# Keys and queries of the next heads transposed ahead of a step's projection matmuls, in a hybrid attention layer

## The chip, the core and the metric

The kernel runs on one core of a Trainium2 chip. The metric is the device time of one execution in microseconds (us), the median over runs. A core has a tensor engine (PE) with a queue for its weight loads (PEld), a vector engine (DVE), a scalar engine (ACT), GpSimd (POOL) and SyncE (SP), which here only issues transfers (DMAs). Each works through its own list of instructions in order and waits for the others by semaphores. PE writes its products into PSUM, eight banks of 128 x 512 float32; DVE and ACT read them from there.

## The reference

One layer of a transformer over 512 tokens of width 1024, in float32:

```python
x = x + 0.5 * swiglu_ffn(x, g1, ...)
h = rms_norm(x, g_mix)
(fq, fk, fv, ff, dq, dk, dv, iq, ik, iw, ga, gb) = split_columns(h @ w_in)
# branch A, 8 heads of 64 (FoX): q, k normed per head,
#   softmax(q.k / 8 + decay of the forget gates, causal) @ v
# branch B, 8 heads of 64 (DSA), one shared key and value head: the same with a relative bias,
#   over the 128 keys that an indexer (iq, ik, iw) picks for each query
merged = sigmoid(ga) * (o_a @ w_branch_a) + sigmoid(gb) * (o_b @ w_branch_b)
x = x + merged @ w_out
x = x + 0.5 * swiglu_ffn(x, g2, ...)
```

## The kernel before

The time goes through five stages: the first feed-forward block, the head of the projection by `w_in` with the indexer's scores, the sixteen attention heads, the merge with `w_out`, and the second feed-forward block. A float32 product is made from three matmuls on operands split in a high and a low part (`mm3`, lines 141 to 143: high times high, low times high, high times low). The high part is a cast on ACT, the low part a difference on DVE.

The order of PE's instructions is the order in which the code is written (`manual_schedule` for PE). The order on ACT, DVE, POOL and SP is set by a scheduler that simulates the program as it is built; so a change in PE's order may change theirs. The scheduler also deals out the tiles to the banks of a tag.

The attention loop (line 1011) goes over 16 heads g: 0 to 7 are FoX, 8 to 15 DSA. A head has four steps s, one for each block of 128 queries, the longest block (512 keys) first. A step holds, in order on PE:

- `value_step` (line 919), for an earlier head's probabilities: `flip` transposes up to four 128x128 tiles p into the PSUM tile pt (L886), ACT casts it to ph (L890), DVE writes the low part pl (L891); then `weigh` multiplies the ph and pl of the flip before with the values (L896, L897).
- `softmax_block` (line 868): scores ps_qk (L579, L580); DVE adds the bias and takes the minimum mn (L875), ACT makes the exponential (L877), DVE the reciprocal rs (L878), POOL scales p (L879).
- `prod.run(FILL[g], ...)`: the fill, some two us of matmuls of the rest of the projection (and, in later heads, of the branch product and the gates), written as units that give up control every few matmuls. Weights are cast to wh (L130) and wl (L136) for it. A finished unit is read out of PSUM: normed queries and keys kn (L650 on ACT, then L546, L548, L549, and POOL), values fv (L663, L664), branch products, gates.
- behind the fill: `get_bias` of the next head (a DMA on SP, L943) at s = 0, and, at odd heads only, `get_k` of the next pair of heads at s = 0 and `get_q` at s = 1.

`get_k` (line 924) does anything only for the heads below 8, so at g = 1, 3 and 5 (and once ahead of the loop). It transposes four tiles kn into the PSUM tile ps_k (L557), and for each half of 64 partitions ACT writes kh (L540) and DVE kl (L541), and two DMAs on SP (L937) copy them to the other 64 partitions. `get_q` does it at g = 1, 3, ..., 13: four transposes into ps_q (L557), and for each half ACT writes st (L570) and DVE the other half of st (L571). In both, ACT and DVE take turns on the one tile: the first half's DVE instruction is over before ACT starts on the second half.

PSUM is full: three banks of tag "acc" for the products, two of tag "s" for the scores, one for the outputs po ("pv"), and two of tag "pt", in which ps_k, ps_q and all the pt of the flips take turns.

Of the kernel before, what the change touches and what calls it, by code (L numbers as in the profile page):

```python
# [35 lines left out]
H = 8  # L36
# [15 lines left out]
def tile_hybrid_layer(ctx: ExitStack, tc: tile.TileContext, a: dict):  # L52
# [467 lines left out]
    with (tc.tile_pool(name="mix", bufs=1) as mp, ExitStack() as att_ctx,  # L520
# [18 lines left out]
        def evac_split(ps, g, hi, lo):  # L539
            S.mul(hi, ps, g)  # L540
            V.scalar_tensor_tensor(lo, ps, g, hi.bitcast(F32), op0=OP.mult, op1=OP.subtract)  # L541
# [18 lines left out]
        def stack_split(ps, g, nm):  # L560

            out = []
            for hf in range(2):
                own, oth = slice(hf * DH, hf * DH + DH), slice(DH - hf * DH, P - hf * DH)
                st = at.tile([P, T], F32R, tag=nm[hf], bufs=2, name="st")
                if g is None:
                    S.copy(st[own], ps[own])
                    V.tensor_sub(st[oth], ps[own], st[own].bitcast(F32))
                else:
                    S.mul(st[own], ps[own], g[own])  # L570
                    V.scalar_tensor_tensor(st[oth], ps[own], g[own], st[own].bitcast(F32),  # L571
                                           op0=OP.mult, op1=OP.subtract)
                out.append(st)
            return out

        def stack_mm(out, st, k, i, n):

            b = slice(i * P, (i + 1) * P)
            PE.matmul(out[:, :n], st[:, b], k[0][:, :n], start=True, stop=False)  # L579
            PE.matmul(out[:, :n], st[:, b], k[1][:, :n], start=False, stop=True)  # L580
# [256 lines left out]
        def topk_run(n):  # L837

            nonlocal topk_debt
            topk_debt += n  # L840
            with tc.issue_after(anchor[0].ins) if anchor[0] else nullcontext():
                while topk_debt >= 1:
                    next(topk, 0)
                    topk_debt -= 1
# [23 lines left out]
        def softmax_block(g, i, q, k, bias, pr, st):  # L868
            n = P * (i + 1)
            b = bias(i)  # L870
            ps = psum.tile([P, T], F32, tag="s", bufs=2, name="ps_qk")
            stack_mm(ps, q[g % 2], k[g % 2], i, n)
            p = at.tile([P, n], F32, tag=f"p{i}", bufs=2, name="p")
            mn, rs = st[0][:, i:i + 1], st[1][:, i:i + 1]
            anchor[0] = V.tensor_tensor_reduce(out=p, in0=ps[:, :n], in1=b, scale=1.0, scalar=3e38,  # L875
                                               op0=OP.add, op1=OP.min, accum_out=mn)
            S.activation(p, p, AF.Exp, bias=mn, scale=-1.0, accum_out=rs)  # L877
            V.reciprocal(rs, rs)  # L878
            G.tensor_scalar(p, p, rs, 1.0, op0=OP.mult, op1=OP.mult)  # L879
            pr[i] = p  # L880
# [32 lines left out]
        def columns(tiles, c, name):  # L913
            return transposed(lambda t: tiles[t // 2][:, t % 2, c * P:(c + 1) * P], name)

        def get_q(g):

            nm, c = ("fq", g // 2) if g < H else ("dq", g // 2 - 4)
            prod.finish(upto[f"{nm}{c // 2}"])
            gain = gq[:, 0:1] if g < H else gq[:, 1:2]  # L920
            return stack_split(columns(tn[f"{nm}{c // 2}"], c % 2, "ps_q"), gain, ("qh", "ql"))

        def get_k(g):

            if g >= H:
                return [(dkh, dkl)] * 2
            c = g // 2
            prod.finish(upto[f"fk{c // 2}"])
            ps = columns(tn[f"fk{c // 2}"], c % 2, "ps_k")
            gain = hg[:, 2:3]  # L930
            out = []
            for hf in range(2):
                own, oth = slice(hf * DH, hf * DH + DH), slice(DH - hf * DH, P - hf * DH)
                hi, lo = k = [mp.tile([P, T], F32R, tag=tag, bufs=3, name=tag) for tag in ("kh", "kl")]
                evac_split(ps[own], gain[own], hi[own], lo[own])
                for t in k:
                    nc.sync.dma_start(t[oth].bitcast(F32), t[own].bitcast(F32))  # L937
                out.append(k)
            return out

        def get_bias(g):
            cb = at.tile([P, T], F32, tag="cb", bufs=2, name="cb")
            nc.sync.dma_start(cb, cum_rows[g:g + 1, :].to_broadcast([P, T]) if g < H else a["rel"][g - H])  # L943

            def bias(i):
                n = P * (i + 1)
                b = tmp_tile("b")
                if g < H:
                    G.tensor_scalar(b[:, :n], cb[:, :n], 1.0, ncum[:, i, g:g + 1], op0=OP.mult, op1=OP.add)
                    G.affine_select(out=b[:, i * P:n], in_=b[:, i * P:n], compare_op=OP.is_ge, fill=BIG, base=0,  # L950
                                    pattern=[[-1, P]], channel_multiplier=1)
                else:
                    G.tensor_sub(b[:, :n], sc[i] if i else cpos, cb[:, T - n:T])
                return b[:, :n]
            return bias
# [6 lines left out]
        for step in range(30):  # L962
            prod.run(MM, upto["fv0"])
            topk_run(TOPK_PRE)
            if step == 5:
                nk = get_k(0)
            if step == 10:
                next(later[1], 0)
            if step == 15:
                nq = get_q(0)  # L970
# [10 lines left out]
        def value_step(g, j):  # L981

            nonlocal flipped, po
            new = (g, j, *flip(j, probs[g])) if g < 2 * H else None
            if flipped:
                fg, fj, ph, pl = flipped
                if fj == 0:

                    po = acc_tile("po") if fg > H and fg % 2 else psum.tile([P, T], F32, tag="pv", name="po")
                if fg < H:  # L990
                    if fj == 0 and fg == 4:
                        prod.finish(upto["fv1"])
                    weigh(po, fj, fv[fj, fg // 4][:, fg % 4], ph, pl)
                else:
                    weigh(po, fj, dvv[:, fj], ph, pl)
                if fj == NT - 1:
                    if fg in (H, H + 2):

                        if fg > H:
                            prod.finish(upto["ba7"])  # L1000
                        for part, nm in zip(oB, ("oh", "ol")):
                            part += [mp.tile([P, T], F32R, tag=f"{nm}{c}", name="oB") for c in range(1, 4)] if fg > H else [
                                mp.tile([P, T], F32R, tag="k" + nm[1], bufs=3, name="oB")]
                    head_out(fg, po, oA if fg < H else oB)
            flipped = new

        def limit(g, s):

            return upto["dq1"] if g < 6 else upto["ga7"] if 4 * g + s < 4 * 9 + 2 else len(units)

        for g in range(2 * H):
            q, k, bias = nq, nk, nb
            probs[g] = [None] * NT
            st = [small.tile([P, NT], F32, tag=nm, name=nm) for nm in ("mn", "rs")]
            for s in range(NT):
                vg, vj = (g - 1, s - 1) if s else (g - 2, NT - 1)
                if vg >= 0:
                    value_step(vg, vj)
                topk_run(TOPK_BEAT)
                softmax_block(g, NT - 1 - s, q, k, bias, probs[g], st)  # L1020
                prod.run(FILL[g], limit(g, s))
                topk_run(TOPK_BEAT)
                if g == H - 1 and s == NT - 1:
                    for _ in topk:
                        pass
                if g + 1 < 2 * H:
                    if s == 0:
                        nb = get_bias(g + 1)
                    if s == 0 and g % 2:
                        nk = get_k(g + 1)  # L1030
                    if s == 1 and g % 2:
                        nq = get_q(g + 1)
                if g == 2 * H - 2:
                    ga[s] = mp.tile([P, T], F32, tag="tn", bufs=8, name="ga")
                    nc.sync.dma_start(ga[s], kept[:, s])
# [127 lines left out]
```

## Time and profile before

| | |
|---|---|
| median of 3 runs | 1089.55 us (1089.39 to 1089.67) |
| span of the profiled execution | 1087.8 us |
| instructions in it | 17784 |
| PE's clock as granted | 9 tenths or more in each of the 40 slices |
| DMA, mean over the span | 118 GB/s |

The page gives only a span for the profiled execution, from its first instruction to its last; the runs' times also hold what lies around it, 1089.55 - 1087.8 = 1.75 us if the profiled execution was like the median one. In a row of a time line stand the start, the duration, the engine, the line, the operation, output and inputs, partitions by elements and the count; in brackets how long the engine was idle before it and what ended the wait. In a row of the waits stand the total in us, the number of times and the longest. Matmuls are pipelined: the next starts before the one before has ended, so a duration of 0.28 us for a 256-wide matmul goes with a start every 0.12 us.

### The profile page before, as it was taken

To read this page: it belongs to the slowest core of one execution; us is meant where nothing else is said; L and a number is where in the kernel's file an instruction comes from. 1 tells how busy PE (TensorE), PEld (TensorE's weight loads), DVE (VectorE), ACT (ScalarE), POOL (GpSimd) and SP (SyncE) were. 2 spreads that over 40 slices of the span, in tenths; PEclk is the share of its full clock that TensorE was granted. 3 is DMA by queue.
4 is the path that set the end of the run, shared out by engine and by line. 5 is a ranking of instruction groups with operands and counts; after the bars stand their busy time and mean duration, and the time that the engine had idled before them with its cause. 6 is when DMAs were issued, how large, how long until landed. Compare 5 with 4: busy or idle time off the path is not lost.

```text
span 1087.8 us, 17784 instructions
## 1 busy us (share of the span) xinstructions
PE 1071.0 (98%) x6808; PEld 963.3 (89%) x6808; DVE 791.2 (73%) x1286; ACT 570.6 (52%) x916; POOL 197.6 (18%) x265
## 2 busy tenths in 40 slices
PE   8999999999999999999999999999999999999998
PEld 6889989998998889999878788788889989989997
DVE  5888767856967579976776765954888758766963
ACT  6635533633555676467766656543635624533550
POOL 1100000100000014367786562000100000000000
PEclk9999999999999999999999999999999999999999
DMA  7554433443442258733323321533544442533441
GB/s 225 134 155 124 110 117 116 112 121 104 125 122 83 84 126 185 207 105 99 87 59 105 123 74 49 165 97 97 126 136 131 125 118 93 136 104 110 126 113 72
DMA packets 45444, 127.87 MB, mean 118 GB/s; under 512 B 5544, under 2 KB 5928, under 8 KB 45360
## 3 DMA queue, kind: packets, MB, share of 16 engines
q1 hardware_dynamic: 38880, 110.22, 33.1%
q0 software_dynamic: 6336, 16.26, 8.2%
q8 instruction: 54, 0.88, 0.3%
q10 hardware_dynamic: 144, 0.26, 0.1%
q14 instruction: 30, 0.25, 0.1%
HBM read 104.94 MB, written 3.42 MB: 100 GB/s over the span
## 4 chain that ended last, share of the span: by engine, by line
PE 53%; DVE 5%; ACT 3%; POOL 3%; issue 2%; DMA 0%; DVEq 0%; POOLq 0%; ACTq 0%
PE pd L142 4%; PE pd L143 4%; PE pd L141 4%; PE ps_f L141 3%; PE ps_f L142 3%; PE ps_f L143 3%; PE pB L142 2%; PE pB L141 2%; PE pB L143 2%; PE ps_t L141 2%; PE ps_t L142 2%; PE ps_t L143 2%; PE pC L142 2%; PE pA L142 2%; PE pA L141 2%
## 5 line engine op out<-in xcount | busy, mean ns | idle before, releaser
L142 PE MATMUL pd<-al,wh 128*128 128x512 f32 (+1 forms) x358 | 138.3, 386 | 1.0 <-DVE al L217 1.0
L141 PE MATMUL pd<-ah,wh 128*128 128x512 f32 (+1 forms) x358 | 138.2, 386 | 0.0
L143 PE MATMUL pd<-ah,wl 128*128 128x512 f32 (+1 forms) x358 | 138.0, 386 | 0.0
L215 POOL DMA_DIRECT2D al<-gu x24 | 20.5, 854 | 490.2 <-ACT al L214 490.2
L112 ACT CAST wh<-s 128x1024 fp32r<-128x1024 f32 x54 | 57.0, 1055 | 92.4 <-PE pB L142 45.9
L419 DVE SCALAR_TENSOR_TENSOR x<-pd,x 128x512 f32<-128x512 f32 (+1 forms) x65 | 44.2, 680 | 62.0 <-PE pd L143 61.8
L141 PE MATMUL ps_t<-wh,xh 128*128 128x256 f32 (+1 forms) x288 | 80.7, 280 | 0.0
L142 PEld LDWEIGHTS pd<-al,wh 128*128 128x128 f32 x358 | 67.2, 188 | 15.0 <-DVE al L217 1.7
L142 PE MATMUL ps_t<-wl,xh 128*128 128x256 f32 (+1 forms) x288 | 80.3, 279 | 0.0
L143 PE MATMUL pB<-tbh,wl 128*128 128x256 f32 x288 | 80.3, 279 | 0.0
L141 PE MATMUL pB<-tbh,wh 128*128 128x256 f32 x288 | 80.3, 279 | 0.0
L142 PE MATMUL pB<-tbl,wh 128*128 128x256 f32 x288 | 80.3, 279 | 0.0
L143 PE MATMUL ps_t<-wh,xl 128*128 128x256 f32 (+1 forms) x288 | 80.2, 279 | 0.0
L141 PEld LDWEIGHTS pd<-ah,wh 128*128 128x128 f32 x358 | 67.3, 188 | 13.6 <-ACT ah L212 0.3
L143 PEld LDWEIGHTS pd<-ah,wl 128*128 128x128 f32 x358 | 67.3, 188 | 13.4
L117 DVE TENSOR_TENSOR wl<-s,wh 128x1024 fp32r<-128x1024 f32 x54 | 65.8, 1218 | 4.2 <-ACT wh L112 3.8
L141 PE MATMUL ps_f<-xh,wh 128*128 128x512 f32 x152 | 60.5, 398 | 0.0
L143 PE MATMUL ps_f<-xh,wl 128*128 128x512 f32 x152 | 59.6, 392 | 0.0
L142 PE MATMUL ps_f<-xl,wh 128*128 128x512 f32 x152 | 59.6, 392 | 0.0
L112 ACT CAST wh<-re 128x1024 fp32r<-128x1024 f32 (+2 forms) x30 | 28.5, 951 | 55.4 <-PE pd L142 15.5
L112 ACT CAST wh<-ra 128x1024 fp32r<-128x1024 f32 (+2 forms) x32 | 29.8, 930 | 48.8 <-PE pd L142 18.7
L141 PEld LDWEIGHTS ps_t<-wh,xh 128*128 128x128 f32 x288 | 54.3, 189 | 0.5
(329 smaller groups left out, 3485.9 us busy)
## 6 DMA issues: line engine op xcount, KB each, us to landing
rb<-in_w_pair_dram SPq DMA_DIRECT2D x16, 512.0 KB, 3.7
re<-in_w_pair_dram SPq DMA_DIRECT2D x16, 512.0 KB, 3.7
rc<-in_w_pair_dram SPq DMA_DIRECT2D x14, 512.0 KB, 3.7
ra<-in_w_pair_dram SPq DMA_DIRECT2D x14, 512.0 KB, 3.6
rd<-in_w_pair_dram SPq DMA_DIRECT2D x12, 512.0 KB, 3.7
al<-gu POOLq DMA_DIRECT2D x24, 256.0 KB, 4.0
rd<-in_w_down_dram SPq DMA_DIRECT2D x12, 384.0 KB, 3.1
rc<-in_w_down_dram SPq DMA_DIRECT2D x10, 384.0 KB, 3.3
```

Source lines behind the costliest of these rows:

```text
L112: S.copy(wh[:, :f], raw[:, :f])
L117: V.tensor_sub(wl[:, :f], raw[:, :f], wh[:, :f].bitcast(F32))
L141: PE.matmul(out, lh, rh, start=start, stop=False, **more)
L142: PE.matmul(out, lh, rl, start=False, stop=False, **more)
L143: PE.matmul(out, ll, rh, start=False, stop=stop, **more)
L215: G.dma_start(l, u, accum_op=OP.add)
L419: V.scalar_tensor_tensor(x[d][:, cols], ps, 0.5, x[d][:, cols], op0=OP.mult, op1=OP.add)
```

## The change

`get_k` and `get_q` are called between a step's softmax block and its fill, no longer behind the fill. `get_bias` stays behind the fill. The amounts of fill, the tiles and the arithmetic stay the same.

```diff
@@ -1018,6 +1018,11 @@
                     value_step(vg, vj)
                 topk_run(TOPK_BEAT)
                 softmax_block(g, NT - 1 - s, q, k, bias, probs[g], st)
+                if g + 1 < 2 * H and g % 2:
+                    if s == 0:
+                        nk = get_k(g + 1)
+                    if s == 1:
+                        nq = get_q(g + 1)
                 prod.run(FILL[g], limit(g, s))
                 topk_run(TOPK_BEAT)
                 if g == H - 1 and s == NT - 1:
@@ -1026,10 +1031,6 @@
                 if g + 1 < 2 * H:
                     if s == 0:
                         nb = get_bias(g + 1)
-                    if s == 0 and g % 2:
-                        nk = get_k(g + 1)
-                    if s == 1 and g % 2:
-                        nq = get_q(g + 1)
```

Ten groups of four transposes move on PE: three ps_k and seven ps_q. On PE, in head 1 at step 0 (ps_t is the projection's product, ident the identity matrix that makes a matmul a transpose):

```order
 L580 MATMUL ps_qk<-kl,st 128x512
-L141 MATMUL ps_t<-wh,xh 128x256
-L142 MATMUL ps_t<-wl,xh 128x256
-L143 MATMUL ps_t<-wh,xl 128x256
...
 L557 MATMUL ps_k<-ident,kn 128x128 x4
+L141 MATMUL ps_t<-wh,xh 128x256
+L142 MATMUL ps_t<-wl,xh 128x256
+L143 MATMUL ps_t<-wh,xl 128x256
...
 L886 MATMUL pt<-ident,p 128x128 x4
```

All 21 matmuls of this step's fill stand behind the four transposes now. ps_q moves in the same way past the fill of step 1. The scheduler deals out the "pt" banks anew in heads 1, 3 and 5: before, ps_q took the bank of the flip of step 1, and the flip of step 2 that of ps_k; now ps_q takes ps_k's, and the flip of step 2 that of the flip of step 1.

On ACT, at the same place of head 1, before (kh is read from ps_k, ph from the flip of step 1, kn from the projection, wh<-rc is the cast of a weight tile):

```order
L877 ACTIVATE p,rs<-p,mn 128x512
L130 CAST wh<-rc 128x1024
L650 ACTIVATE kn<-ps_t,rstd 128x256 x2
L540 ACTIVATE kh<-ps_k,hg 64x512
L890 CAST ph<-pt 128x512
L546 ACTIVATE sqh<-kn 128x512
L540 ACTIVATE kh<-ps_k,hg 64x512
```

and now:

```order
L540 ACTIVATE kh<-ps_k,hg 64x512
L877 ACTIVATE p,rs<-p,mn 128x512
L130 CAST wh<-rc 128x1024
L650 ACTIVATE kn<-ps_t,rstd 128x256 x2
L540 ACTIVATE kh<-ps_k,hg 64x512
L890 CAST ph<-pt 128x512
```

The first kh has moved ahead of the exponential, the second stands behind the weight cast and the two kn, as the first did before. Head 5 reads alike (kh, wh, kn x2, exponential, kh); in head 3 both kh stand ahead of ph with only the exponential between them.

On DVE, in head 11 at steps 1 and 2 (p and mn of L875 are the softmax's, st the low part of the next queries, pl the low part of the flip of step 2; wl<-rc is the pass that makes the low part of a weight tile):

```order
+L571 SCALAR_TENSOR_TENSOR st<-ps_q,gq,st 64x512
 L136 TENSOR_TENSOR wl<-rc,wh 128x1024
...
 L571 SCALAR_TENSOR_TENSOR st<-ps_q,gq,st 64x512
 L891 TENSOR_TENSOR pl<-pt,ph 128x384
...
-L571 SCALAR_TENSOR_TENSOR st<-ps_q,gq,st 64x512
 L891 TENSOR_TENSOR pl<-pt,ph 128x256
```

Before, one st stood ahead of this pl and one behind it; now the first is ahead of the weight pass and the second ahead of pl. In head 13 it is the same about pl, and in head 7 the second st has moved ahead of a score pass (L875).

On SP, the copies of the keys (L937) of heads 3 and 5 now stand ahead of the DMA of get_bias, and those of heads 1 and 5 partly ahead of a weight load (L129).

## The prediction

> **What bounds the kernel now.** I read the page first, then the waits of the tensor engine (PE), then how busy each engine is in the stretch where the attention heads run, and last the time lines of PE, ACT and DVE around the moved transposes.
>
> ```profile
> span 1087.8 us, 17784 instructions
> PE 1071.0 (98%) x6808; PEld 963.3 (89%) x6808; DVE 791.2 (73%) x1286; ACT 570.6 (52%) x916; POOL 197.6 (18%) x265
> ```
>
> ```profile
> sum 195.00, PE 188.79 PEld 168.89 DVE 146.97 ACT 132.25 POOL 127.33; mean PE 31.47 PEld 28.15 DVE 24.49 ACT 22.04 POOL 21.22
> ```
>
> The second view covers 440 to 635 us, which holds every instruction that the change moves. PE is idle there for 195.00 - 188.79 = 6.2 us. The change neither adds nor removes a matmul, so PE's work stays as it is, and the most that any new order could give is these 6.2 us, of which the change can touch only what hangs on the moved transposes. In the waits of PE these are such rows:
>
> ```profile
> PE pt L886 <- DVE kl L541: 1.7, 3, 1.1
> PE ps_q L557 <- DVE pl L891: 0.5, 1, 0.5
> PE pt L886 <- DVE st L571: 0.3, 1, 0.3
> ```
>
> The first row: three times (heads 1, 3 and 5) the probability transposes of step 2 (tile pt) wait until DVE has written the second low part kl of the next keys. Both the tile of transposed keys, ps_k, and pt come from the tag "pt", which has two PSUM banks; PE can't write the bank before the last reader has left it. The reading of one such tile is a chain of four:
>
> ```profile
> L540 ACT ACTIVATE kh<-ps_k,hg x8: 677/682/685, 439.2 to 529.2; 64x512 fp32r<-64x512 f32 x8
> L541 DVE SCALAR_TENSOR_TENSOR kl<-ps_k,hg,kh x8: 734/750/757, 440.4 to 529.9; 64x512 fp32r<-64x512 f32 x8
> ```
>
> kh of the first half, its kl, kh of the second half, its kl: 2 x (0.68 + 0.75) = 2.86 us when nothing stands between them. How much time passes on PE between the transposes, head 1:
>
> ```profile
> 468.49 0.28 PE L141 MATMUL ps_t<-wh,xh 128*128 128x256 f32 x1
> ...
> 470.82 0.28 PE L143 MATMUL ps_t<-wh,xl 128*128 128x256 f32 x1
> 470.94 0.60 PE L557 MATMUL ps_k<-ident,kn 128*128 128x128 f32 x4
> 471.38 0.60 PE L886 MATMUL pt<-ident,p 128*128 128x128 f32 x4
> ...
> 472.17 0.28 PE L141 MATMUL ps_t<-wh,xh 128*128 128x256 f32 x1
> ...
> 474.62 0.60 PE L557 MATMUL ps_q<-ident,kn 128*128 128x128 f32 x4
> 475.60 0.55 PE L886 MATMUL pt<-ident,p 128*128 128x128 f32 x3 [0.38 <-DVE kl L541]
> ```
>
> The 21 projection matmuls of step 0 start from 468.49 to 470.82, one every (470.82 - 468.49) / 20 = 0.117 us. Four transposes hold PE for 471.38 - 470.94 = 0.44 us. All that follows is reckoned from start to start, since the ends of matmuls in the profile overlap the next start.
>
> **The change part by part.** *What is removed.* If the moved transposes waited for nothing and made nothing wait, the gaps of today would go. Head 1: pt would start at 474.62 + 0.44 = 475.06 and not at 475.60: 0.54 us. Heads 3 and 5:
>
> ```profile
> 501.14 0.28 PE L141 MATMUL ps_t<-wh,xh 128*128 128x256 f32 x1
> ...
> 503.25 0.60 PE L557 MATMUL ps_q<-ident,kn 128*128 128x128 f32 x4
> 504.16 0.55 PE L886 MATMUL pt<-ident,p 128*128 128x128 f32 x3 [0.31 <-DVE kl L541]
> ```
>
> ```profile
> 523.39 0.28 PE L141 MATMUL ps_t<-wh,xh 128*128 128x256 f32 x1
> ...
> 526.60 0.28 PE L141 MATMUL ps_t<-wh,xh 128*128 128x256 f32 x1
> ...
> 528.24 0.28 PE L143 MATMUL ps_t<-wh,xl 128*128 128x256 f32 x1
> 529.03 0.66 PE L557 MATMUL ps_q<-ident,kn 128*128 128x128 f32 x4 [0.51 <-DVE pl L891]
> 530.74 0.55 PE L886 MATMUL pt<-ident,p 128*128 128x128 f32 x3 [1.06 <-DVE kl L541]
> ```
>
> Head 3: 504.16 - 503.25 - 0.44 = 0.47. Head 5: 529.03 - (528.24 + 0.12) = 0.67 in front of ps_q, and 530.74 - 529.03 - 0.44 = 1.27 in front of pt. Together 2.95 us.
>
> *What is added.* With the new order the distance from ps_k to ps_q on PE hardly changes: before it is ps_k, flip, scores, fill of step 1, ps_q (474.62 - 470.94 = 3.68 us in head 1); now it is ps_k, fill of step 0, flip, scores, ps_q (472.17 - 468.49 = 3.68, since ps_k's 0.44 comes in and stays in front of the same start, 472.17). But the banks are dealt out anew: before, ps_q goes where the flip of step 1 was (it waits for pl) and only the flip behind it needs ps_k's bank. Now ps_q itself goes into ps_k's bank and waits for the second kl, with a whole step's fill queued behind it, and the flip of step 2 goes where the flip of step 1 was. So the chain of four must be over 3.68 us after ps_k began where today it has until the flip of step 2 (475.60). What ACT has to do inside this chain, head 1:
>
> ```profile
> 469.53 0.72 ACT L877 ACTIVATE p<-p,mn 128x512 f32<-128x512 f32 x1 [0.47 <-DVE mn L875]
> ...
> 470.44 1.05 ACT L130 CAST wh<-rc 128x1024 fp32r<-128x1024 f32 x1
> 471.39 0.83 ACT L650 ACTIVATE kn<-ps_t,rstd 128x256 f32<-128x256 f32 x2
> 472.12 0.68 ACT L540 ACTIVATE kh<-ps_k,hg 64x512 fp32r<-64x512 f32 x1
> ```
>
> ```profile
> 499.16 0.60 PE L557 MATMUL ps_k<-ident,kn 128*128 128x128 f32 x4
> ```
>
> ```profile
> 498.42 0.73 ACT L877 ACTIVATE p<-p,mn 128x512 f32<-128x512 f32 x1 [0.97 <-DVE mn L875]
> ...
> 499.80 0.68 ACT L540 ACTIVATE kh<-ps_k,hg 64x512 fp32r<-64x512 f32 x1 [0.56 <-PE ps_k L557]
> ```
>
> A free ACT starts kh 499.80 - 499.16 = 0.64 us after the first transpose. ACT's new order in head 1 is kh, exponential of 512, weight cast wh, two kn, kh.
>
> Head 1, step by step: ps_k starts at 468.49 (where the fill stood). First kh 469.13 to 469.81, first kl to 470.56; the exponential to about 470.6; the cast wh at 470.88, taking it that it moves with the fill in front of it (today's 470.44 + 0.44), or at 470.7 if ACT alone held it; it ends at 471.9. Two kn take 472.12 - 471.39 = 0.73, so the second kh runs from 472.6 to 473.3, its kl to 474.05. ps_q could start at 472.17 and starts at 474.1. Behind it 0.44 of transposes and 474.62 - 472.17 = 2.45 of fill: the flip of step 2 starts at 476.99 where it started at 475.60. That is +1.4 us (+1.2 with the earlier cast; -0.54 if the second kh came before the cast, which would end the chain at 472.0).
>
> Head 3: ACT's order has no cast there. ps_k starts 18 matmuls earlier than 499.16, at 497.05; kh to 498.4, exponential to 499.15 with its sum read by 499.25, kh to 499.9, kl to 500.7: ps_q, due at 501.14, waits for nothing, and the 0.47 goes. The values fv (lines 663 and 664) of the projection that ends in this fill come 0.44 later and behind one more write of the queries, so that pl of step 2 comes about 0.6 later and the matmul on it (line 897) gives back about 0.55. Net +0.1, with -0.5 (nothing given back) and +0.3 (the full 0.75 of a DVE write, from the row of kl) as bounds.
>
> Head 5:
>
> ```profile
> 523.94 1.05 ACT L130 CAST wh<-rc 128x1024 fp32r<-128x1024 f32 x1 [0.68 <-PE ps_t L143]
> 524.90 0.83 ACT L650 ACTIVATE kn<-ps_t,rstd 128x256 f32<-128x256 f32 x2
> ```
>
> ps_k starts at 523.39, kh runs from 524.03 to 524.71, and the cast, ready before, stands behind it until 525.76; two kn to 526.5, exponential to 527.2, second kh to 527.9, kl to 528.65. ps_q is due at 526.60 and starts at about 528.7, 2.1 late. The flip then starts at 528.7 + 0.44 + (528.24 + 0.12 - 526.60) = 530.9, today 530.74: +0.1. The old waits, 0.67 + 1.27, become one of 2.1 (bounds -1.9, if the chain ran ahead of the cast, and +0.4).
>
> Heads 7 to 13 move queries alone, no ps_k; ps_q's bank is free. What changes is DVE's order: in heads 11 and 13 the second query write st now stands ahead of pl of step 2, in head 7 ahead of a score pass.
>
> ```profile
> 607.02 0.74 DVE L571 SCALAR_TENSOR_TENSOR st<-ps_q,gq,st 64x512 fp32r<-64x512 f32 x1
> 607.80 0.56 DVE L891 TENSOR_TENSOR pl<-pt,ph 128x384 fp32r<-128x384 f32 x1
> ```
>
> ```profile
> 608.50 0.41 PE L886 MATMUL pt<-ident,p 128*128 128x128 f32 x2 [0.50 <-DVE rs L878]
> ```
>
> In head 11 pl ends at 608.36 and the next flip starts 0.14 later: DVE is late there today (rs is a small reciprocal that it does right behind pl). One more st ahead of pl could cost 0.75 in each of three heads; st1 in turn moves ahead of the weight pass, into time in which DVE may be idle. I take +0.2 for all, nearer to nothing, with -0.2 and +2.25 as ends.
>
> The keys' copies on SP (line 937) are issued up to 2.9 us earlier, in head 5 ahead of one weight load. That is hidden: each such weight tile is loaded long before its cast, the one below 26 us before the cast at 523.94. The bias load get_bias stays behind the fill; it is passed by the key copies at heads 3 and 5, whose triggers come before the fill ends, so I cost it at nothing; without that cover it would hold the first score pass of the next head.
>
> ```profile
> 497.80 0.33 SPq L129 DMA_DIRECT2D rc<-in_w_ga_dram  x1
> ```
>
> *Sum:* 1.4 + 0.1 + 0.1 + 0.2 = +1.8 us on a span of 1087.8, that is 1089.6; the median of the runs, 1089.55, stands 1.75 above this profiled span, so the forecast is 1089.55 + 1.8 = 1091.3 us.
>
> The rows of waits above can be weighed against two rules. The Trainium skill, "Perfetto Trace Analysis", section Matmuls, says that independent matmul groups should go through different PSUM banks so that the emptying of one overlaps the next group; the change does that for ps_k and the fill behind it, and by this rule alone the 2.95 us would be gained. The same page, section Optimization Strategy, says that a gap that repeats can mean that there is too little PSUM for the next tile; with two banks for three tiles the gap then only moves. The trace agrees with the second so far as every one of the gaps in these heads ends with a reader leaving a "pt" bank.
>
> **The rivals.** *The gaps really go* (chance 0.18). The chains finish before ps_q is due, because the scheduler's instructions on ACT turn out to be free in time (the second kh ahead of the cast, or the cast not held by the fill). For it: head 3 gets through by my own reckoning. Against it: ACT is in order, and 1.05 + 0.73 us of cast and kn stand between the two kh in heads 1 and 5. Full size 1089.55 - 2.95 = 1086.6 us.
>
> *No net change* (0.17). PE loses at ps_q what it gains at the flip, and the 1.4 of head 1 is smaller because later waits on other engines shrink when PE comes later (POOL's p, for one). It gives 1089.6 us, within -1.3 and +0.5.
>
> *Slower through DVE* (0.15). The second st ahead of pl in heads 11 and 13, and ahead of the score pass in head 7, is pushed on to PE in full, 3 x 0.75 = 2.25, in place of the 0.2: +1.6 + 2.25 = 3.9, 1093.4 us. It decides when DVE has no idle time between the scores of step 1 and pl of step 2, so that an earlier st delays all behind it. Against it: DVE is busy 146.97 of 195.00 us there.
>
> That the change does nothing is excluded: ten groups of transposes stand elsewhere on PE, and what waits for ps_k's bank is another instruction.
>
> **How the numbers follow.** The forecast case, +0.5 to +3.0, has 0.50. A measurement of this kernel can tell about 0.2% or 2.2 us from no change. Faster by more than that needs three quarters of the whole 2.95: 0.13 of the gain rival's 0.18. Slower by more: the rival through DVE, 0.15, and the part of the forecast case above +2.2, 0.20, in which head 1 loses its 1.4, head 5 its upper end and the DSA heads half a microsecond. The rest, 0.30 + 0.17 + 0.05, is within 0.2%. The range leaves out 0.13 below, the gain rival nearly in full, so from -2.1 (1087.4), and about 0.07 above, the worse half of the DVE rival, so to +4.2 (1093.8).
>
> **What would show it.** Right: ps_q in heads 1 and 5 waits for kl L541, near 1.9 and 2.1 us, with ACT's second kh behind the cast wh and the two kn; in head 3 there is no wait on kl; the flips of step 2 wait for no kl. The gain rival shows no PE wait on kl at all and a span under 1086. The DVE rival shows waits of over half a microsecond in heads 7, 11 and 13 on pl or mn. The step that I trust least is the cast's place in head 1: were the second kh to end before 471.5, the forecast would fall by over 1 us, and were the net of heads 7 to 13 over 1 us of either sign, the sum would be wrong however right the rest.

## The result and the profile after

| | before | after |
|---|---|---|
| median of 5 runs each, us | 1089.55 (1089.03 to 1091.68) | 1095.61 (1093.99 to 1097.48) |
| span of the profiled execution, us | 1087.8 | 1093.2 |

The ratio is 1.0052 [1.0041, 1.0063]: slower by 5.7 us [4.5, 6.9]. The forecast was +1.8, with 1093.8 as the upper end of its range; the median lies 1.8 us above that end.

The page of after, its first two lines, and the sum over the stretch of the heads:

```profile
span 1093.2 us, 17786 instructions
PE 1072.1 (98%) x6808; PEld 964.8 (88%) x6808; DVE 791.6 (72%) x1286; ACT 571.0 (52%) x916; POOL 196.7 (18%) x265
```

```profile
sum 200.00, PE 189.27 PEld 169.37 DVE 147.68 ACT 131.66 POOL 126.68; mean PE 189.27 PEld 169.37 DVE 147.68 ACT 131.66 POOL 126.68
```

The stretch (440 to 640 us, 5 us longer than the one shown of before) has 200.00 - 189.27 = 10.7 us without PE work where before had 6.2. The matmuls are the same, and most of the time went into waits; what went into a slower clock counts as busy and stands under head 5. The waits of PE there:

```profile
PE ps_q L557 <- DVE kl L541: 3.6, 2, 2.0
PE ps_f L142 <- DVE oAl L911: 2.2, 1, 2.2
PE pt L886 <- POOL p L879: 1.8, 3, 0.8
PE pt L886 <- DVE st L571: 1.5, 2, 1.2
```

The row of before "pt L886 <- DVE kl L541: 1.7" is gone, and in its place stand the two waits that the prediction named, in heads 1 and 5. The second row is new and was not foreseen: in head 9 a matmul of the fill (ps_f, the branch product) waits 2.2 us for oAl, the low part of branch A's output.

Where the 5.4 us of the two profiled executions arise is read by taking the same matmul in both time lines, its start in the one less its start in before (us; the score matmuls L579 of 512 keys up to head 6, the 512-wide L896 behind that). E4, E6 and E8 are experiments told below; E8 moves the keys and queries of the FoX heads only, E4 and E6 the queries of the DSA heads and head 7 only.

| place, by its time in before | after | E8 | E4 | E6 |
|---|---|---|---|---|
| 468.0, head 1 begins | -0.74 | -0.22 | +1.97 | +0.19 |
| 483.3, head 2 begins | +1.62 | +1.15 | | |
| 511.3, head 4 begins | +1.54 | +1.03 | | |
| 536.8, head 6 begins | +3.26 | +1.22 | +1.98 | +0.42 |
| 579.1, ahead of the wait in head 9 | +3.07 | | +1.95 | +0.45 |
| 592.6, behind it | +4.70 | | +5.08 | +0.47 |
| 617.7, behind head 11 | +4.39 | | +4.75 | +0.17 |
| 642.6, behind head 13 | +5.36 | | +5.78 | +1.13 |

What stands at a column's first row is a difference of the executions ahead of anything moved, so only the steps from row to row count. Between 536.8 and 579.1, where head 7's queries move, E4 and E6 lose nothing. In after: head 1 +2.36, head 3 -0.08, head 5 +1.72, heads 6 to 8 -0.19, head 9 +1.63, head 11 -0.31, head 13 +0.97.

**Head 1** goes as the prediction had it. The time line of PE, then of ACT:

```profile
467.51 0.40 PE L580 MATMUL ps_qk<-kl,st 128*128 128x512 f32 x1
467.74 0.60 PE L557 MATMUL ps_k<-ident,kn 128*128 128x128 f32 x4
...
471.54 0.66 PE L886 MATMUL pt<-ident,p 128*128 128x128 f32 x4 [0.74 <-POOL p L879]
...
474.15 0.63 PE L557 MATMUL ps_q<-ident,kn 128*128 128x128 f32 x4 [1.60 <-DVE kl L541]
...
477.07 0.49 PE L886 MATMUL pt<-ident,p 128*128 128x128 f32 x3
```

```profile
468.89 0.67 ACT L540 ACTIVATE kh<-ps_k,hg 64x512 fp32r<-64x512 f32 x1
470.02 0.72 ACT L877 ACTIVATE p<-p,mn 128x512 f32<-128x512 f32 x1 [0.47 <-DVE mn L875]
...
470.74 1.03 ACT L130 CAST wh<-rc 128x1024 fp32r<-128x1024 f32 x1
471.68 0.83 ACT L650 ACTIVATE kn<-ps_t,rstd 128x256 f32<-128x256 f32 x2
472.53 0.68 ACT L540 ACTIVATE kh<-ps_k,hg 64x512 fp32r<-64x512 f32 x1
```

Between the two kh stand the exponential, the cast and both kn; the second kh starts 4.8 us after ps_k began. ps_q waits 1.60 us for the kl behind it, with the fill queued behind it. The 0.74 on POOL's p ahead of it is probably the lead with which this execution came in, lost again. E3, E8 and E10, with the same order on ACT here, have no such wait at this flip, and the lag in head 1 grows by 1.38, 1.37 and 1.37 in them; so 1.4 of after's 2.36 is the change's.

**Head 5** has the wait that was forecast, and something more. The row of PE, and PE, the clock (PEclk, the column behind POOL) and the DMAs in three neighbouring stretches:

```profile
530.29 0.63 PE L557 MATMUL ps_q<-ident,kn 128*128 128x128 f32 x4 [1.96 <-DVE kl L541]
```

```profile
527.73:531.14 3.41, 1.45 (x13) 1.16 (x12) 2.63 (x5) 3.31 (x7) 3.33 (x6) 1.00 0.70 145
531.14:534.55 3.41, 3.41 (x18) 3.41 (x17) 2.03 (x6) 1.98 (x6) 3.23 (x7) 0.50 0.79 219
534.55:537.96 3.41, 3.41 (x29) 3.33 (x28) 2.86 (x5) 2.52 (x6) 3.28 (x4) 1.00 0.02 6
```

In the first stretch PE was busy for 1.45 of 3.41 us; in the next its clock was granted at 0.50, for exactly 3.41 us, and 18 matmuls ran in it where the third stretch has 29. At half the clock 3.41 us hold 1.7 us of full-speed work, so up to 1.7 us are lost. That is the difference between head 5's +1.72 here and its +0.19 in E8, where the clock stayed at 1.00.

**Head 9.** First before, DVE and PE, then after, DVE, POOL and PE:

```profile
579.92 0.91 DVE L136 TENSOR_TENSOR wl<-rc,wh 128x512 fp32r<-128x512 f32 x1
580.86 0.69 DVE L911 TENSOR_TENSOR oAl<-o,oAh 64x512 fp32r<-64x512 f32 x1
...
582.04 0.74 DVE L571 SCALAR_TENSOR_TENSOR st<-ps_q,gq,st 64x512 fp32r<-64x512 f32 x1
```

```profile
581.60 0.50 PE L142 MATMUL ps_f<-oAl,wh 128*128 128x512 f32 x1
```

```profile
583.11 0.74 DVE L571 SCALAR_TENSOR_TENSOR st<-ps_q,gq,st 64x512 fp32r<-64x512 f32 x1
583.88 1.36 DVE L136 TENSOR_TENSOR wl<-rc,wh 128x512 fp32r<-128x512 f32 x1
585.28 1.64 DVE L911 TENSOR_TENSOR oAl<-o,oAh 64x512 fp32r<-64x512 f32 x1
```

```profile
583.40 2.97 POOL L1038 TENSOR_TENSOR ga<-ga,rb 128x512 f32<-128x512 f32 x2
```

```profile
586.97 0.50 PE L142 MATMUL ps_f<-oAl,wh 128*128 128x512 f32 x1 [2.21 <-DVE oAl L911]
```

Before, oAl was written at 581.55 and read at 581.60: just in time, which is why no wait showed there. Now the first query write st stands ahead of it (0.74), and both passes between SBUF tiles run beside GpSimd's products of the gates (ga): wl takes 1.36 instead of 0.91 and oAl 1.64 instead of 0.69. 0.74 + 0.45 + 0.95 = 2.14 us, and PE waits 2.21.

### The profile page after: what moved, and what is told of

Same layout as the page of the kernel before. It is cut to its first block, busy times and chain, and to the rows that moved or that the text cites. A ratio compares the mean times of both kernels' runs of the same rounds, so it can differ in the third digit from the quotient of the medians.

```text
span 1093.2 us, 17786 instructions
## 1 busy us (share of the span) xinstructions
PE 1072.1 (98%) x6808; PEld 964.8 (88%) x6808; DVE 791.6 (72%) x1286; ACT 571.0 (52%) x916; POOL 196.7 (18%) x265
## 4 chain that ended last, share of the span: by engine, by line
PE 51%; DVE 5%; ACT 3%; POOL 3%; issue 3%; DMA 1%; DVEq 0%; POOLq 0%; SPq 0%; ACTq 0%
PE pd L142 4%; PE pd L143 4%; PE pd L141 4%; PE ps_f L142 3%; PE ps_f L141 3%; PE ps_f L143 3%; PE pB L142 2%; PE pB L143 2%; PE pB L141 2%; PE pA L142 2%; PE pC L142 2%; PE pC L143 2%; PE pA L143 2%; PE pA L141 2%; PE pC L141 2%
## 5 line engine op out<-in xcount | busy, mean ns | idle before, releaser
L142 PEld LDWEIGHTS ps_t<-wl,xh 128*128 128x128 f32 x288 | 54.8, 190 | 0.3
```

The lines of the kernel that those rows point to most:

```text
L142: PE.matmul(out, lh, rl, start=False, stop=False, **more)
```

## The experiments

Each edit is made to the kernel before; "in front" is the place ahead of the fill. Differences in us are the ratio's, by about 1090. H is 8.

**E1, the keys alone in front.**

```diff
+                if s == 0 and g + 1 < 2 * H and g % 2:
+                    nk = get_k(g + 1)
                 prod.run(FILL[g], limit(g, s))
...
-                    if s == 0 and g % 2:
-                        nk = get_k(g + 1)
```

> Only the keys' transposes are moved ahead of the fill; the queries' stay behind it. Theory of places (each wait is where a tile's reading chain is not over when PE needs its bank or its result): ps_k is read during two fills, about 6 us, so that ps_q and the flip of step 2 in heads 1, 3 and 5 wait for nothing, and heads 7 to 13 stay as before: 1 to 3 us faster than before. Theory of the keys' chain (moving ps_k itself disturbs ACT and costs the time): slower than before by 1 us or more. Theory of the clock (halved clock windows make most of the loss): no window is halved if no PE wait is near 2 us.

Measured: 1088.31 us, ratio 0.9986 [0.9978, 0.9995], 1.5 us faster than before. **E2, the queries alone in front:**

```diff
+                if s == 1 and g + 1 < 2 * H and g % 2:
+                    nq = get_q(g + 1)
                 prod.run(FILL[g], limit(g, s))
...
-                    if s == 1 and g % 2:
-                        nq = get_q(g + 1)
```

> Only the queries' transposes are moved; the keys' stay behind the fill. Theory of places: in heads 1, 3 and 5 ps_q now comes 0.6 us after the flip of step 1 and goes into that flip's bank, so it waits for the flip's pl, some 1 to 2 us each time; head 9 loses about 1.6 us (oAl behind st on DVE) as the whole change does: 5 to 9 us slower than before. Theory of the keys' chain: less than 2 us slower. Theory of the clock: the loss goes with the number of halved windows in the record.

Measured: 1097.05 us, 1.0067 [1.0054, 1.0079], +7.3. The waits of E1 that name kl, and the first waits of E2:

```profile
PE ps_q L557 <- DVE kl L541: 0.2, 1, 0.2
```

```profile
PE ps_q L557 <- DVE pl L891: 5.0, 3, 2.3
PE ps_f L142 <- DVE oAl L911: 2.2, 1, 2.2
```

So the two halves of the change are of opposite sign. That -1.5 + 7.3 = +5.8 meets the whole is no proof that the whole is made of these two losses: E2 waits for pl where after waits for kl, and in E2's profile the clock is halved three times in the heads, in after's once. In E1 ps_k has one fill more for its chain and ps_q stays behind its own fill: the waits shrink to 0.2. In E2 ps_q follows the flip of its own step with nothing but the scores between, and waits for that flip's pl in heads 1, 3 and 5.

**E3, both in front in the FoX heads 1, 3 and 5 only; E4, the queries in front in heads 7 to 13 only.** In front of the fill:

```diff
+                if s == 0 and g + 1 < 2 * H and g % 2 and g < H - 1:
+                    nk = get_k(g + 1)
+                if s == 1 and g + 1 < 2 * H and g % 2 and g < H - 1:
+                    nq = get_q(g + 1)
```

```diff
+                if s == 1 and g + 1 < 2 * H and g % 2 and g > H - 2:
+                    nq = get_q(g + 1)
```

> Both are moved, but only in the FoX heads 1, 3 and 5. Theory of places: head 1 loses 2.2, head 3 nothing, head 5 0.4 without and 1.5 with a halved clock window: 2.5 to 4 us slower than before, ps_q waiting for kl about 2 us in heads 1 and 5. Theory that the DSA heads make the loss: within 1 us of before. Theory of the clock: slower by 1.1 to 1.7 us for each halved window, and hardly slower without one.

> Only the queries in heads 7, 9, 11 and 13 are moved. Theory of places: head 9 loses 1.6 us to the wait of the projection matmul for oAl, heads 7, 11 and 13 together 0 to 0.8: 1.6 to 2.4 us slower than before. Theory that the FoX heads make all the loss, and head 9's wait only follows from the delay before it: within 0.7 us of before. E3's and E4's losses add up to that of the whole change if the places are independent.

Measured: E3 1092.6 us, 1.0027 [1.0017, 1.0037], +2.9; E4 1094.04 us, 1.0039 [1.0027, 1.0051], +4.3. E4 is the larger, in the heads for which the forecast had 0.2. (The sum, 7.2, is above the whole, 5.7; both intervals are wide enough for it.) E4's profile has head 9's wait on oAl, 2.13 us, and the clock behind it (the second pair); the first pair is another halving, ahead of anything moved:

```profile
432.69:436.10 3.41, 3.41 (x27) 3.19 (x26) 3.38 (x13) 2.77 (x5) 2.53 (x3) 1.00 0.35 71
436.10:439.51 3.41, 3.41 (x10) 2.63 (x9) 3.41 (x11) 0.00 (x0) 1.55 (x3) 0.50 0.89 195
...
582.87:586.28 3.41, 1.28 (x6) 0.77 (x5) 3.35 (x6) 0.69 (x3) 2.57 (x3) 1.00 0.44 127
586.28:589.69 3.41, 3.41 (x12) 2.84 (x12) 2.24 (x7) 2.06 (x5) 1.16 (x2) 0.50 0.09 10
```

At 436 us E4's lag jumps from +0.36 to +1.97, so this execution lost 1.6 us to the clock that are not the change's, and by the lags the heads cost it 5.78 - 1.95 = 3.8. How much of E4's +4.3 comes from such windows is not known: of its five runs the one at full clock took 1091.42 us, and the four others ran at a mean clock of 0.997, which is two halved windows each.

**E5, only the queries of head 9 in front** (`g == 9` in E4's condition):

> Only head 9's query transposes are moved. Theory of places: the projection matmul's wait for oAl (about 2 us, two thirds of a microsecond of it given back at the next flip) is all that counts of the DSA heads: 1.6 us slower than before in a run without a halved clock window and about 2.5 with one behind the wait. Rival (heads 7, 11 and 13 carry half of E4's loss): under 1.5 us slower.

Measured: 1093.12 us, 1.0027 [1.0015, 1.0039], +2.9. One group of four transposes in one head costs more than the whole forecast. Its profile has the same single wait (2.19 us on oAl) and, behind it, the same halved clock; the lag grows by 3.2 in head 9. The medians leave 4.3 - 2.9 = 1.4 for heads 7, 11 and 13 together, with intervals of over 1 us to each side on both numbers; E4's lags give 0.0, -0.3 and +1.0.

**E6, E4 with GpSimd's gate products held back** behind the last scaling of p (L879), so that they no longer lie beside wl and oAl; DVE's order there is that of E4.

```diff
-            G.tensor_scalar(p, p, rs, 1.0, op0=OP.mult, op1=OP.mult)
+            scaled[0] = G.tensor_scalar(p, p, rs, 1.0, op0=OP.mult, op1=OP.mult)
...
-        for d in range(4):
-            G.tensor_mul(ga[d], ga[d], rb)
+        with tc.issue_after(scaled[0].ins):
+            for d in range(4):
+                G.tensor_mul(ga[d], ga[d], rb)
```

> As E4, but GpSimd's four products ga*rb are held back until it has scaled the last head's probabilities; DVE's list around oAl stays as in E4 (st, weight pass, oAl). Theory that GpSimd beside DVE stretches the passes on two SBUF tiles (weight pass 0.91 to 1.36 us, oAl 0.69 to 1.64): both are short again, the wait for oAl falls from 2.1 to about 0.7, no window is halved behind it, and of E4's loss at most 1.5 us stays. Rival (the order on DVE alone makes the wait: st ahead of oAl): the wait stays near 2 us and the time near E4's.

Measured: 1090.27 us, 1.0006 [0.9998, 1.0015], +0.7 where E4 had +4.3. DVE and PE in head 9 (L912 is L911 of the other kernels):

```profile
580.49 0.74 DVE L571 SCALAR_TENSOR_TENSOR st<-ps_q,gq,st 64x512 fp32r<-64x512 f32 x1
581.27 0.69 DVE L136 TENSOR_TENSOR wl<-rc,wh 128x512 fp32r<-128x512 f32 x1
581.99 0.69 DVE L912 TENSOR_TENSOR oAl<-o,oAh 64x512 fp32r<-64x512 f32 x1
```

```profile
582.73 0.50 PE L142 MATMUL ps_f<-oAl,wh 128*128 128x512 f32 x1 [0.60 <-DVE oAl L912]
```

Without GpSimd beside them wl and oAl are back at 0.69 each. The wait is 0.60, about what st alone costs, and the matmuls behind get even that back: E6's lag is +0.45 ahead of head 9 and +0.47 behind it. So head 9's +3 is shown to hang on GpSimd's stretching, and st without it costs nothing there. The Trainium skill, "SBUF — State Buffer", section Who interferes with whom, says that a DVE instruction with two SBUF inputs contends with a GpSimd instruction that reads SBUF, by an exclusive lock; the trace agrees: wl and oAl, two SBUF inputs each, go from 0.69 to 1.36 and 1.64, while st, which reads PSUM, takes 0.74 beside GpSimd as well as without it. What E6 still loses, +0.96 by the lag, is head 13. There PE and DVE in before, then in E6:

```profile
633.49 0.41 PE L886 MATMUL pt<-ident,p 128*128 128x128 f32 x2 [0.42 <-DVE rs L878]
633.50 0.75 DVE L571 SCALAR_TENSOR_TENSOR st<-ps_q,gq,st 64x512 fp32r<-64x512 f32 x1
```

```profile
633.53 0.76 DVE L571 SCALAR_TENSOR_TENSOR st<-ps_q,gq,st 64x512 fp32r<-64x512 f32 x1
634.32 0.56 DVE L892 TENSOR_TENSOR pl<-pt,ph 128x384 fp32r<-128x384 f32 x1
634.44 0.41 PE L887 MATMUL pt<-ident,p 128*128 128x128 f32 x2 [1.21 <-DVE st L571]
```

The second st, the last reader of ps_q, runs at the same time in both. In before the flip of step 3 (two tiles) started ahead of it, so the flip can't have needed ps_q's bank; in E6 it waits 1.21 us for this st and starts while pl of step 2 still reads the other bank. With two banks for the tag, the flip of step 3 must have been dealt ps_q's bank now. The profile prints no bank numbers; this is read from the times. So head 13 is once more a wait for a bank, as in the FoX heads. The prediction's rival through DVE looked for waits on pl or mn, and the longest of these are the same in E6 as in before, 0.5 and 0.6 us.

**E7, E3 with ps_k copied to SBUF first** (heads 1, 3 and 5), kh and kl made from the copy: the bank is free after one ACT instruction, without the chain of four.

```diff
+            if g:
+                kc = tmp_tile("kc")
+                S.copy(kc, ps)
+                ps = kc
```

> As E3, but ACT copies the transposed keys out of their PSUM bank in one instruction (0.6 to 0.7 us), and kh and kl are made from the copy in SBUF. Theory that the chain of four in the bank, with ACT's cast between, makes the waits of ps_q: the bank is free 1.3 us after the transposes, ps_q waits for nothing, no window is halved, and the time is 1 to 2.5 us below before's, 4 to 5 below E3's. Rival (the place of the transposes or ACT's load makes the loss): no more than 1 us below E3.

Measured: 1092.12 us, 1.0019 [1.0009, 1.0029], +2.1 where a gain was expected; against E3's +2.9 the intervals overlap. ps_q does not wait any more, so the bank was what it waited for, and in head 1 the loss of 1.4 is gone (the lag goes from -0.69 to -0.81). But ACT in head 5, and PE:

```profile
525.30 1.04 ACT L130 CAST wh<-rc 128x1024 fp32r<-128x1024 f32 x1
526.23 0.83 ACT L650 ACTIVATE kn<-ps_t,rstd 128x256 f32<-128x256 f32 x2
526.96 1.46 ACT L540 ACTIVATE kh<-kc,hg 64x512 fp32r<-64x512 f32 x2
528.44 0.58 ACT L890 CAST ph<-pt 128x512 fp32r<-128x512 f32 x1
```

```profile
530.01 0.55 PE L886 MATMUL pt<-ident,p 128*128 128x128 f32 x3 [1.51 <-DVE pl L891]
```

Both kh now stand behind the wh and the kn and ahead of ph, and the next flip waits 1.51 us for the pl made from that ph. In head 5 the bank was the form of the wait; ACT's list between the two transposes is what fills the time. PE's waits for POOL's p also grow, from 1.1 us in all in E3 to 2.6, which was not followed further. My theory was half right.

**E8, E3 with PE kept busy while ps_q waits:** seven 512-wide matmuls, whose result nothing reads, ahead of ps_q in heads 1 and 5. This adds work and takes no wait's cause away; only the idle time is filled.

```diff
+                    if g in (1, 5):
+                        busy = acc_tile("busy")
+                        for _ in range(7):
+                            PE.matmul(busy, xh[0][:, :P], xh[0], start=True, stop=True)
                     nq = get_q(g + 1)
```

> As E3, with seven matmuls of 128x512 that nothing reads put ahead of ps_q in heads 1 and 5 (1.6 us of work in a wait of about 2). Theory that idle time inside one window of 3.4 us halves the clock in the next: PE is not idle there, the clock is whole in every run, and the time is about 1 us below E3's, near the fastest of its runs (1.5 us above before or less). Rival (the halved windows have another cause, or cost nothing): time and clock as in E3, or more by the added work.

Measured: 1091.16 us, 1.0013 [1.0005, 1.0022], +1.4, which is 1.5 less than E3 with 14 matmuls more (the intervals, [0.5, 2.4] and [1.9, 4.0], overlap). E3 and E8 over the same 35 us of heads 3 to 5:

```profile
500.00:535.00 35.00, 32.28 (x241) 30.44 (x241) 23.86 (x59) 26.30 (x59) 24.40 (x41) 0.95 0.37 112
```

```profile
500.00:535.00 35.00, 33.89 (x261) 31.85 (x261) 25.14 (x62) 27.07 (x61) 24.41 (x41) 1.00 0.39 113
```

The clock is 0.95 in E3 (3.41 us at a half) and 1.00 in E8. The chain itself is as late as in E3: the flip of step 2 comes +1.6 after its place in both. So the idle time of a wait costs twice, once as itself and once through the clock behind it, and the second part is shown here by itself: head 5 costs 1.74 by the lag in E3 and 0.19 in E8, and the other heads the same in both. That the clock would be whole in every run was wrong: eight of E8's twelve runs have a mean clock of 0.998, one halved window, as many runs of before have (E3's are at 0.995 to 0.999).

**E9, E1 with E6's held products; E10, the whole change with E8's matmuls and E6's held products.** Nothing else is edited.

> E1 (only the keys are moved) with GpSimd's four products ga*rb held back to the end of the heads, as in E6. Theory that GpSimd stretches DVE's passes beside it: the flips of step 3 in heads 9, 11 and 13, which wait 1.4 us in all in E1 for DVE, wait less, and the time is 0.5 to 1.5 us below E1's, 2 to 3 below before's. Rival (those waits have another cause, or the products are missed later): as E1, or slower.

> The whole change, with both cures: matmuls that nothing reads keep PE busy ahead of ps_q in heads 1 and 5 (E8), and GpSimd's products ga*rb are held back (E6). If the two together are what the forecast of 1.8 us left out, this kernel is 1 to 2.5 us slower than before and 3.5 to 4.5 faster than the change without them. If something else adds to the loss, it stays 3 us or more above before.

Measured: E9 1088.83 us, 0.9987 [0.9978, 0.9996], -1.4: no better than E1, so holding the products is worth nothing where no st stands ahead of oAl, and the further gain that I expected did not come. E10 1091.65 us, 1.0017 [1.0008, 1.0026], +1.9, where the whole change has +5.7. Of its waits, those that name st, kl or oAl:

```profile
PE pt L887 <- DVE st L571: 1.5, 2, 1.2
PE ps_q L557 <- DVE kl L541: 0.7, 2, 0.4
PE ps_f L142 <- DVE oAl L912: 0.6, 1, 0.6
```

With the two things that the forecast did not hold taken out, the change costs what the forecast said. That it meets +1.8 to a tenth is luck (the interval is 0.9 to 2.8): by the lags of its profile heads 1, 3 and 5 cost 1.4, -0.1 and 0.2, near the forecast's 1.4, 0.1 and 0.1, but heads 6 to 8 give back 0.2, and heads 9, 11 and 13 cost 0.0, -0.3 and +1.0 where the forecast had 0.2 for all of them.

## Why the prediction was wrong

**Right: heads 1, 3 and 5 as a chain.** The second kh of head 1 was put at 472.6 and ran from 472.53; ps_q was put at 474.1 and started at 474.15; the flip of step 2 at 476.99, and it started at 477.07. (The lead of 0.74 and the wait of 0.74 on POOL cancel, so the agreement is not all merit; in E8, without either to speak of, the flip comes 1.6 later than in before, forecast 1.4. And the first kl, put at 469.8, ran only from 471.17; that cost nothing, since ACT was at the cast and the kn until 472.5.) In head 3 no kl is waited for, 0.5 is gained and 0.4 given back in E8, forecast 0.47 and 0.55. In head 5 ps_q was put at 528.7; it started at 530.29, which less the lag of 1.57 at the scores ahead of it is 528.72. The sum of the FoX heads was 1.4 + 0.1 + 0.1 = 1.6; E8 measured +1.4 [0.5, 2.4]. The key copies on SP cost nothing: E1 moves them likewise and is faster. Of the two rules weighed there, E1 bears out the one on banks and after the one on gaps that move.

**Wrong: the clock, costed at nothing.** The page showed it at nine tenths or more in every slice, and the sum went by start-to-start times at that clock. But the forecast itself put two waits of about 2 us on PE in heads 1 and 5. In head 5 this halved the clock for 3.41 us: +1.5 (E3 against E8). In head 9 the same happens behind the oAl wait in E4 and E5: between the matmuls at 579 and 593 E4 loses 3.13 us, where the wait is 2.13.

**Wrong: "I take +0.2 for all" in heads 7 to 13.** E4 measured +4.3 [2.9, 5.6], and in after's time line heads 9 to 13 cost 1.63 - 0.31 + 0.97 = 2.3; the prediction itself said that a net of over 1 us here would make its sum wrong. The step looked at what stands ahead of pl and of a score pass, the rows of the order's difference in heads 7, 11 and 13. In head 9 the first st also moved ahead, of a weight pass and of oAl, and I didn't ask who reads oAl: a matmul of the fill, due 0.05 us after it was written. And I took the passes' durations as fixed, although the wl in head 9 of before already took 0.91, not 0.69, beside a pass of GpSimd. In the lags of E4, head 9 costs 3.13, head 11 gains 0.33 and head 13 costs 1.03. Head 13's part was missed for another reason: the step took it that without a ps_k only DVE's order changes, but the flip of step 3 now waits for ps_q's bank (E6).

In after's profiled execution these make up the sum: 1.4 in head 1, -0.1 in head 3, 1.7 in head 5 (1.5 of it the clock), -0.2 in heads 6 to 8 and 2.3 in heads 9 to 13 are 5.1 of the 5.4.

**The rivals.** The one through DVE had the engine and the sign, and at +3.9 came nearer than the forecast, but not its place or its mechanism: heads 11 and 13 together cost 0.7 of the 1.5 that it gave them, by a bank and not by a late pl, head 7 nothing, and what made E4 dear was head 9 with GpSimd and the clock. The gain rival holds for the keys alone (E1), at half of its 2.95. The upper end, +4.2, left out the worse half of the DVE rival and had no term for the clock at all.

**Open.** Heads 7, 11 and 13 were not run apart (the time lines separate them), what head 11 gains was not sought, nor was E3 plus E4 against the whole settled closer than the intervals. In E9 waits of 1.4 us on the reciprocal rs remain; what sets them was not sought. A second kh ahead of the weight cast, which the prediction put at a gain of 0.54 in head 1, was not tried. The best version run is E1, the keys alone.

## What to carry to other kernels

Moving PE work ahead of other PE work gains only if the readers of the first, on engines that work in order, are through before PE comes back for the buffer: the keys had a whole fill for that and gained, the queries had a flip and some scores and lost. When an order changes on an engine off the critical path, look at every value that is now written later and at how just in time its reader was, not only at the waits that the profile of before shows; and take the durations of passes that will lie beside GpSimd's from such rows. Count a wait of about 2 us on PE at up to nearly twice its length, since the clock behind it may be halved.

## What was not expected of the hardware

The clock halved after waits of only about 2 us. In these profiles every halving in the heads lasted 3.41 us and came behind a window of the same length in which PE was busy for 1.52 us or less. Windows in the heads with more, though the waits were as long, were followed by the full clock, as around the 1.60 of head 1 of after:

```profile
469.71:473.12 3.41, 2.10 (x16) 1.58 (x14) 3.41 (x10) 3.07 (x6) 1.52 (x2) 1.00 0.48 169
473.12:476.53 3.41, 2.38 (x21) 2.41 (x22) 3.23 (x6) 1.99 (x4) 3.39 (x5) 1.00 0.72 194
```

Here the wait falls across the border of two windows, and neither is idle enough; in head 9 of after it is the same, which is why head 9 costs 1.63 there and 3.13 in E4. The emptiest window in the heads that I saw followed by the full clock is one of before, around its two waits in head 5:

```profile
528.00:531.41 3.41, 1.84 (x14) 1.35 (x13) 2.99 (x7) 2.62 (x5) 3.33 (x7) 1.00 0.91 292
```

So in the heads the limit seems to lie between 1.52 and 1.84 us of PE work in a window, and whether a wait is punished depends on where the windows happen to lie, which differs from execution to execution. PE's busy time is not the whole rule, though. Ahead of the heads the clock was halved at 24 us in the profiles of E2, E5, E6, E9 and E10, behind windows with 2.2 to 2.4 us of PE work, and at 436 us in E4 and at 435 us in E10, behind windows in which PE was busy throughout, in E4 for 2.0 of the 3.41 us with matmuls of only 8 columns (L809). What the clock goes by is open.

Halved windows are also part of the spread between runs: after ran at a mean clock of 0.998 to 0.994 and took 1094 to 1097.5 us, E2 took 1094.8 us at 0.998 and 1099.0 at 0.994 (0.0016 of the mean clock is one such window). But before, which has no wait of 2 us in the heads, has runs at 0.998 and 0.997 too, and up to 1092.4 us. The Trainium skill, "TensorE: Matmul & The Clock Gate", Part 1, gives a free-running window of 3413 ns, and the trace agrees: the halved windows of E2 last 3.413 us and begin 132, 149 and 166 such lengths behind the first; that the clock falls after a whole idle window, as it also says, is not what these runs show, since windows in which PE was busy for 1.2 to 1.5 of 3.41 us were enough.
